# A hybrid decoder layer on one core: the softmax division of two blocks at once on GpSimd, q's square there, and the meta weights transposed in one step

## The chip, the cores and the metric

The kernel runs on one core of one Trainium2 chip. The metric is the device time of one execution in microseconds (us). A core has five engines that run side by side, each through its own instructions in order: TensorE (PE; PEld is its weight load), VectorE (DVE), ScalarE (ACT), GpSimd (POOL) and SyncE (SP), which here only starts transfers. They wait for each other through semaphores.

## The reference, cut to what matters here

A layer of 1024 tokens with 16 meta tokens ahead of them: attention and a state-space scan side by side, merged by gates, then a feed-forward part. The change is in the attention, which works on blocks of 128 tokens. Each block looks at the 16 meta tokens, the block before it and itself.

```python
q = rmsnorm(q.reshape(b, L, N_Q_HEADS, HEAD_DIM), q_norm[i])      # 16 heads of 64, 4 for each of 4 k/v heads
k_win = jnp.concatenate([meta k, k_prev, kb], axis=2)             # 16 + 128 + 128 columns
s = jnp.einsum('bnqkrd,bnskd->bnkrqs', qb, k_win) * scale         # masked by the window
m = jnp.maximum(jnp.max(s, axis=-1, keepdims=True), sink)
e = jnp.exp(s - m)
p = e / (jnp.sum(e, axis=-1, keepdims=True) + jnp.exp(sink - m))
o_r = jnp.einsum('bnkrqs,bnskd->bnqkrd', p, v_win)
```

## The kernel before

The program is written in the order of the algorithm. A scheduler puts the instructions of each engine in an order of its own, by their priorities (an instruction written later has less) and by when its own model of times thinks that operands and buffers are there. After that the order on an engine is fixed.

The attention loop (L734 to L740) runs over 32 steps i = kv * 8 + b: for each of the 4 k/v heads the 8 blocks of 128 tokens, each with 4 query heads. Five stages are called in each turn, with a lead in steps: `q_proj` 10, `values` 0, `p_turn` 1, `scores` 4, `q_turn` 6.

- `q_proj` (L609): 24 matmuls of 256 columns into `q`. ScalarE squares them into `qsq` (L619) and copies them into `qp` (L620), VectorE sums the squares by head into `qss` (L621). Every fourth block `rsqrt` (L146) makes 13 small VectorE instructions on 16 numbers (L151 to L159).
- `q_turn` (L628): GpSimd scales q into `qn` (L633), TensorE transposes it, ScalarE and VectorE split it into `qs`, the rounded part and the rest (L645, L648). At a new k/v head `k_prep` (L583) does the same for the keys (`kh`, `kl`).
- `scores` (L652): two matmuls for each head into `s`, then one VectorE instruction (L663) that adds the mask, writes `pr` and leaves the smallest negated value in `mn`. ScalarE takes the exponentials and their sums `den` (L669). VectorE makes `es`, adds it to `den` and takes the reciprocal, four numbers each (L667, L672, L673). Then the weights are divided: heads 0 and 1 on VectorE (L675), heads 2 and 3 on GpSimd in one instruction (L677). `pr` has three buffers.
- `p_turn` (L681): eight transposes of `pr` (`ptp` for the block before, `ptc` for the own one), split by ScalarE and VectorE into `ph` and `pl` (L199, L200). The 16 meta columns are split on GpSimd into `pm` (L701, L702), 48 columns a head with a gap of zeros, transposed head by head (`ptm`, four matmuls), and copied to `pmt` (L707).
- `values` (L710): products with v into `o`, five matmuls of 512 columns, the last with the meta weights, 48 rows high (L720). ScalarE and VectorE join the halves in `av` (L725, L726), and SyncE stores it to `at_d` (L728).

Between the blocks the gate units `g` (24 matmuls of 512 columns, L540) run: four ahead of the loop and one after each of the steps 22, 27 and 31. Weights are split in halves by `w_cols` (L107), the lower half (`wl_q`, `wl_g`, L104) on GpSimd. Behind the loop the memory of attention is given back, SyncE loads `W` (L765), the scan runs on VectorE (L784 to L794), and TensorE runs the other gate units (L767, L798).

Of the kernel before, what the change touches and what calls it, by code (L numbers as in the profile page):

```python
# [46 lines left out]
def hybrid_layer_kernel(ctx: ExitStack, tc: tile.TileContext, x, meta_tokens, norm_mix, w_in, q_norm, k_norm,  # L47
# [174 lines left out]
    vm = kvp.tile([48, NKV, 2, HD], F32R, name="vm")  # L222
# [6 lines left out]
    with sbuf("p1", 2) as p1:  # L229
# [73 lines left out]

        nc.vector.memset(vm.bitcast(F32), 0.0)
        split(vm[0:16, :, 0], vm[0:16, :, 1], o[:NMETA, 256:512].rearrange("p (h d) -> p h d", d=HD))
        nc.vector.tensor_copy(vm[32:48], vm[0:16])
# [252 lines left out]
    with sbuf("ag", 1, "right") as ag, sbuf("at", 2) as at:  # L559
# [12 lines left out]
        pms = []  # L572

# [6 lines left out]

        kt = {}

        def k_prep(kv):  # L583
# [3 lines left out]
            c0 = kv * HD  # L587

# [20 lines left out]
        def q_proj(i):  # L609
# [16 lines left out]
        qst, probs, pts = {}, {}, {}  # L626
# [25 lines left out]
        def scores(i):  # L652
# [4 lines left out]
            mn = at.tile([P, 4], F32, tag="mn", name=f"mn{i}")  # L657
            for h in range(4):
                o = bank(f"s{i}_{h}", "s")
                for j in range(2):  # L660
# [3 lines left out]
                                               scalar=nsink[:, kv * 4 + h:kv * 4 + h + 1], op0=ALU.add, op1=ALU.min, accum_out=mn[:, h:h + 1])  # L664
            es = at.tile([P, 4], F32, tag="es", name=f"es{i}")
            den = at.tile([P, 4], F32, tag="den", name=f"den{i}")
            nc.vector.tensor_tensor(out=es, in0=mn, in1=nsink[:, kv * 4:kv * 4 + 4], op=ALU.subtract)  # L667
            for h in range(4):
                nc.scalar.activation(out=pr[:, h, :n], in_=pr[:, h, :n], func=AF.Exp, scale=-1.0,  # L669
                                     bias=mn[:, h:h + 1], accum_out=den[:, h:h + 1])  # L670
# [3 lines left out]
            for h in range(2):  # L674
                nc.vector.tensor_scalar(out=pr[:, h, :n], in0=pr[:, h, :n], scalar1=den[:, h:h + 1], scalar2=None,  # L675
                                        op0=ALU.mult)
            nc.gpsimd.tensor_tensor(out=pr[:, 2:4, :n], in0=pr[:, 2:4, :n],  # L677
                                    in1=den[:, 2:4].unsqueeze(2).to_broadcast([P, 2, n]), op=ALU.mult)
            probs[i] = pr

        def p_turn(i):  # L681
# [15 lines left out]
            if i < 2:  # L697
                pms.append(one([P, 4, 48], F32R, f"pm{i}"))
                nc.gpsimd.memset(pms[i].bitcast(F32), 0.0)
            pm, src = pms[i % 2], pr[:, :, cm:cm + 16]  # L700
            nc.gpsimd.tensor_copy(pm[:, :, 0:16], src)  # L701
            nc.gpsimd.tensor_tensor(out=pm[:, :, 32:48], in0=src, in1=pm[:, :, 0:16].bitcast(F32), op=ALU.subtract)  # L702
            pt = bank(f"ptm{i}", "x")
            for h in range(4):
                nc.tensor.transpose(pt[:48, h * P:h * P + P], pm[:, h, :].bitcast(F32), ident)
            pmt = at.tile([48, 512], F32R, tag="pmt", name=f"pmt{i}")
            nc.scalar.copy(pmt, pt[:48])  # L707
            pts[i] = parts, pmt

        def values(i):  # L710
            kv, b = divmod(i, 8)
            c0 = kv * HD
# [3 lines left out]
            for k, (kb, ph, pl) in enumerate(parts):  # L716
                nc.tensor.matmul(o, v2[:, kb, kv].rearrange("p a d -> p (a d)"), ph, start=(k == 0), stop=False)
            for kb, ph, pl in parts:
                nc.tensor.matmul(o[:64, :], v2[:, kb, kv, 0, :], pl, start=False, stop=False)
            nc.tensor.matmul(o, vm[:, kv].rearrange("p a d -> p (a d)"), pm, start=False, stop=True)  # L720
# [575 lines left out]
```

## Time and profile before

| | |
|---|---|
| Time, median of 3 runs | 1693.79 us (1693.68 to 1696.36) |
| The profiled execution | 1697.95 us |
| Its span, first to last instruction | 1696.2 us, granted TensorE clock 0.975 |
| TensorE busy | 1586.7 us, 94% of the span |
| VectorE busy | 1181.0 us, 70% |
| ScalarE busy | 695.7 us, 41% |
| GpSimd busy | 372.4 us, 22% |
| Chain that ended last | TensorE 59%, VectorE 14% of the span |

The shares are averages over stages that have different limits. Matmuls are pipelined, so that the busy time of TensorE includes their overlap; how fast it runs is read from how many it issues in a stretch. Times in the rows count from the span's start. A wait is put down to what released it.

### The profile page before, as it was taken

The numbers are of one execution on the slowest core, as the hardware profiler recorded it, in microseconds if no ns is written. First come the engines' busy times: TensorE is split into PE (matmuls) and PEld (weight loads), VectorE is DVE, ScalarE is ACT, GpSimd is POOL, SyncE is SP. The second block draws the span as 40 slices with busy tenths as digits, with TensorE's granted clock in tenths as the row PEclk, the third lists the DMA queues.
The fourth block names the chain that finished last, engine by engine and source line by source line (L and its number), as shares of the span: only waits on it lengthen the run. The fifth ranks groups of instructions, "written<-read, shape, count | busy, mean of one in ns | idle before, by whom it ended". The sixth has DMA issues, their size and how long they took to land.

```text
span 1696.2 us, 22168 instructions
## 1 busy us (share of the span) xinstructions
PE 1586.7 (94%) x8002; PEld 1318.3 (78%) x8002; DVE 1181.0 (70%) x2280; ACT 695.7 (41%) x1363; POOL 372.4 (22%) x277
## 2 busy tenths in 40 slices
PE   7999888989989999799998897999999999799999
PEld 5788768778867888788887785788888888678787
DVE  7779885999995798732217688865656665399763
ACT  4433425878885421442212333533333333243230
POOL 0000112243321001113323200111111121265441
PEclk9999989999999999999999997999999999999999
DMA  5254442011012874742213341423223331584431
GB/s 190 61 130 133 134 143 74 24 38 45 20 51 60 311 218 131 212 130 75 74 51 104 111 163 57 143 87 106 94 94 116 107 106 56 199 305 159 147 109 75
DMA packets 175359, 196.93 MB, mean 116 GB/s; under 512 B 12769, under 2 KB 125409, under 8 KB 175121
## 3 DMA queue, kind: packets, MB, share of 16 engines
q1 hardware_dynamic: 166736, 183.94, 33.6%
q10 hardware_dynamic: 8288, 11.01, 2.1%
q8 instruction: 63, 1.03, 0.3%
q0 software_dynamic: 224, 0.56, 0.1%
q14 instruction: 48, 0.39, 0.1%
HBM read 140.62 MB, written 54.85 MB: 115 GB/s over the span
## 4 chain that ended last, share of the span: by engine, by line
PE 59%; DVE 14%; DMA 4%; ACT 3%; issue 3%; SPq 0%; POOL 0%; ACTq 0%; DVEq 0%
PE ch_fg L907 6%; PE ch_fu L907 6%; PE ch L907 6%; PE za L122 5%; PE wo L122 5%; PE zb L122 5%; PE si L907 4%; PE g L122 3%; PE th_fg L907 3%; PE th_fu L907 3%; PE q L122 2%; PE si_fg L907 2%; PE si_fu L907 2%; DVE pr L663 1%; DVE cm L207 1%
## 5 line engine op out<-in xcount | busy, mean ns | idle before, releaser
L122 PE MATMUL g<-xn,wh_g 128*128 128x512 f32 x512 | 165.4, 403 | 0.1
L907 PE MATMUL ch<-B,A 128*128 128x512 f32 x528 | 127.2, 398 | 13.8 <-ACT B L1228 7.4
L907 PEld LDWEIGHTS ch<-B,A 128*128 128x128 f32 x528 | 100.7, 192 | 37.7 <-ACT B L1228 7.8
L122 PEld LDWEIGHTS g<-xn,wh_g 128*128 128x128 f32 x512 | 97.2, 192 | 22.7 <-PE s L661 0.3
L122 PE MATMUL q<-wh_q,xn 128*128 128x256 f32 x512 | 105.3, 293 | 5.4 <-ACT qp L620 5.4
L122 PE MATMUL g<-xn,wl_g 128*128 128x512 f32 x256 | 102.2, 399 | 0.0
L907 PE MATMUL si<-B,A 128*128 128x512 f32 x396 | 92.6, 389 | 0.5 <-DVE h2o L911 0.5
L122 PE MATMUL wo<-wh_o,mt 128*128 128x512 f32 x256 | 83.9, 406 | 9.3 <-DVE h L984 4.9
L122 PE MATMUL u<-xn,wh_u 128*128 128x272 f32 (+2 forms) x384 | 92.4, 334 | 0.0
L122 PEld LDWEIGHTS q<-wh_q,xn 128*128 128x128 f32 x512 | 85.1, 196 | 7.0 <-ACT qp L620 5.8
L907 PEld LDWEIGHTS si<-B,A 128*128 128x128 f32 x396 | 74.3, 188 | 16.3 <-issue 0.9
L911 POOL TENSOR_TENSOR a<-c,c_fg 128x512 f32<-128x512 f32 x10 | 15.9, 1586 | 315.0 <-DVE c L911 211.1
L858 DVE TENSOR_TENSOR ssm<-za,zs 128x512 f32<-128x512 f32 x16 | 11.0, 690 | 105.3 <-ACT zs L857 105.3
L1228 ACT CAST A<-rawa 128x1536 fp32r<-128x1536 f32 (+1 forms) x28 | 38.5, 1374 | 99.7 <-issue 49.4
L122 PE MATMUL zb<-zt,wh_zb 128*128 128x512 f32 x256 | 79.3, 390 | 0.0
L122 PE MATMUL za<-zt,wh_za 128*128 128x512 f32 x256 | 79.2, 390 | 0.0
L122 PE MATMUL q<-wl_q,xn 128*128 128x256 f32 x256 | 74.5, 291 | 0.0
L911 DVE TENSOR_TENSOR A<-rawa,A 128x1536 fp32r<-128x1536 f32 (+1 forms) x28 | 65.4, 2334 | 12.5 <-ACT A L1228 12.5
L911 POOL TENSOR_TENSOR B<-t,B 128x1536 fp32r<-128x1536 f32 (+1 forms) x16 | 60.2, 3774 | 54.5 <-ACT B L1228 54.5
L669 ACT ACTIVATE pr<-pr,mn 128x272 f32<-128x272 f32 (+1 forms) x128 | 64.8, 507 | 16.5 <-DVE mn L663 14.0
L122 PEld LDWEIGHTS u<-xn,wh_u 128*128 128x128 f32 x384 | 66.7, 198 | 5.5
L122 PEld LDWEIGHTS wo<-wh_o,mt 128*128 128x128 f32 x256 | 50.0, 196 | 20.5 <-DVE h L984 5.3
(426 smaller groups left out, 4211.6 us busy)
## 6 DMA issues: line engine op xcount, KB each, us to landing
rawa<-act_d SPq DMA_DIRECT2D x21, 768.0 KB
raw_fg<-in_w_ffn_in_dram SPq DMA_DIRECT2D x20, 512.0 KB
raw_fu<-in_w_ffn_in_dram SPq DMA_DIRECT2D x20, 512.0 KB
rawb<-in_w_ffn_out_dram SPq DMA_DIRECT2D x6, 1536.0 KB
act_d<-a SPq DMA_DIRECT2D x33, 256.0 KB
raw_g<-in_w_in_dram SPq DMA_DIRECT2D x16, 512.0 KB
act_d<-c_fg SPq DMA_DIRECT2D x30, 256.0 KB
u_d<-uf SPq DMA_DIRECT2D x64, 65.0 KB
```

The source lines that it names most:

```text
L122: nc.tensor.matmul(o, lhs(kb, a), rhs(kb, b), start=(kb == 0 and i == 0), stop=(kb == n - 1 and i == 2))
L207: nc.vector.tensor_tensor(out=m, in0=v, in1=a[:, 2 * k:2 * k + 2, g0:g0 + 4].unsqueeze(3) .to_broadcast([P, 2, 4, n]), op=ALU.mult)
L663: nc.vector.tensor_tensor_reduce(out=pr[:, h, :n], in0=o[:, :n], in1=mask, scale=1.0, scalar=nsink[:, kv * 4 + h:kv * 4 + h + 1], op0=ALU. ...
L669: nc.scalar.activation(out=pr[:, h, :n], in_=pr[:, h, :n], func=AF.Exp, scale=-1.0, bias=mn[:, h:h + 1], accum_out=den[:, h:h + 1])
L858: nc.vector.tensor_tensor(out=dst, in0=oa, in1=sg, op=ALU.mult)
L907: nc.tensor.matmul(o, lhs(kb, a), rhs(kb, b), start=(first and kb == 0 and i == 0), stop=(kb == n - 1 and i == 2), skip_group_check=not first)
L911: eng.tensor_tensor(out=out, in0=in0, in1=in1, op=op)
L1228: nc.scalar.copy(hi, src)
```

## The change

- The division by `den` waits for two blocks (an even one and the odd one after it). `mn`, `es` and `den` are tiles of 2 x 4 numbers, `es`, the addition and the reciprocal run once for the pair, and GpSimd then divides all four heads of the first and of the second block, one instruction each. VectorE divides nothing.
- q's square is taken on GpSimd from `qp`, and VectorE scales its sums by 1/64 once for four blocks.
- The meta weights of the four heads lie side by side in `pm` (4 x 2 x 16 columns, the rounded part and the rest), and one transpose turns them. In `values` each head then multiplies them with a tile `vms` of v's meta rows that is zero outside the rows of this head: four matmuls of 128 columns. GpSimd fills `vms` at each new k/v head from `v1`, whose second half a DMA on GpSimd's queue copies.
- The lower part of the weights, `pl`, is multiplied with both halves of v (128 columns instead of 64).
- All stages but `q_proj` get a priority 1000 higher.

```diff
+        vms = [one([P, 4, 2, HD], F32R, f"vm{i}") for i in range(2)]
+        for vm in vms:
+            nc.gpsimd.memset(vm.bitcast(F32), 0.0)
...
+            for h in range(4):
+                nc.gpsimd.tensor_copy(vms[kv % 2][32 * h:32 * h + 32, h], v1[:, kv])
...
-            nc.scalar.activation(out=sq, in_=o[:, 0:256], func=AF.Square, scale=0.125)
-            nc.scalar.copy(qp[i // 4][:, b % 4, :], o[:, 0:256])
+            q_ = qp[i // 4][:, b % 4, :]
+            nc.scalar.copy(q_, o[:, 0:256])
+            nc.gpsimd.tensor_tensor(out=sq, in0=q_, in1=q_, op=ALU.mult)
...
-                qr[i // 4] = rsqrt(qss.pop(i // 4), P, 16, at, f"q{i}")
+                ms = qss.pop(i // 4)
+                nc.vector.tensor_scalar(out=ms, in0=ms, scalar1=1.0 / HD, scalar2=None, op0=ALU.mult)
+                qr[i // 4] = rsqrt(ms, P, 16, at, f"q{i}")
...
+            if b % 2 == 0:
+                sums[i // 2] = [at.tile([P, 2, 4], F32, tag=t, name=f"{t}{i}") for t in ("mn", "es", "den")]
+            mn, es, den = sums[i // 2]
...
+            probs[i] = pr
+            if b % 2 == 0:
+                return
...
-            for h in range(2):
-                nc.vector.tensor_scalar(out=pr[:, h, :n], in0=pr[:, h, :n], scalar1=den[:, h:h + 1], scalar2=None,
-                                        op0=ALU.mult)
-            nc.gpsimd.tensor_tensor(out=pr[:, 2:4, :n], in0=pr[:, 2:4, :n],
-                                    in1=den[:, 2:4].unsqueeze(2).to_broadcast([P, 2, n]), op=ALU.mult)
-            probs[i] = pr
+            for k in range(2):
+                pr, n = probs[i - 1 + k], window(b - 1 + k)[1]
+                nc.gpsimd.tensor_tensor(out=pr[:, :, :n], in0=pr[:, :, :n],
+                                        in1=den[:, k].unsqueeze(2).to_broadcast([P, 4, n]), op=ALU.mult)
...
-            for h in range(4):
-                nc.tensor.transpose(pt[:48, h * P:h * P + P], pm[:, h, :].bitcast(F32), ident)
-            pmt = at.tile([48, 512], F32R, tag="pmt", name=f"pmt{i}")
-            nc.scalar.copy(pmt, pt[:48])
+            nc.tensor.transpose(pt[:, 0:P], pm.bitcast(F32).rearrange("p h a k -> p (h a k)"), ident)
+            pmt = at.tile([P, P], F32R, tag="pmt", name=f"pmt{i}")
+            nc.scalar.copy(pmt, pt[:, 0:P])
...
-            nc.tensor.matmul(o, vm[:, kv].rearrange("p a d -> p (a d)"), pm, start=False, stop=True)
+            for h in range(4):
+                nc.tensor.matmul(o[:, h * P:h * P + P], vms[kv % 2][:, h].rearrange("p a d -> p (a d)"), pm, start=False,
+                                 stop=True, skip_group_check=True)
...
-                    f(i + ahead)
+
+                    with ExitStack() as first:
+                        if f is not q_proj:
+                            first.enter_context(tc.high_priority(1000))
+                        f(i + ahead)
```

How the scheduler lays this out is seen at two places in the middle of attention. A name's number is its step, so `pr10` is the weights of step 10. GpSimd before, at the division of steps 10 and 11 (`pm0` and `pm1` were two tiles used in turn):

```order
L677 TENSOR_TENSOR pr10_3809<-pr10_3809,den10_3828 128x544
L701 CAST pm0_2959<-pr10_3809 128x4x16
L702 TENSOR_TENSOR pm0_2959<-pr10_3809,pm0_2959 128x4x16
L633 TENSOR_TENSOR qn15_4173<-qp12_3246,rs_i_q15_3633 128x256
L677 TENSOR_TENSOR pr11_3909<-pr11_3909,den11_3928 128x544
L701 CAST pm1_3068<-pr11_3909 128x4x16
L702 TENSOR_TENSOR pm1_3068<-pr11_3909,pm1_3068 128x4x16
```

GpSimd with the change, at the same two steps (here and below its lines are those of the changed program; L688 is the division, L708 and L709 make `pm`, L623 is q's square, L638 makes `qn`):

```order
L688 TENSOR_TENSOR pr10_3770<-pr10_3770,den10_3773 128x1088
L688 TENSOR_TENSOR pr11_3864<-pr11_3864,den10_3773 128x1088
L708 CAST pm10_4082<-pr10_3770 128x4x16
L638 TENSOR_TENSOR qn16_4251<-qp16_3699,rs_i_q19_4035 128x256
L638 TENSOR_TENSOR qn17_4357<-qp16_3699,rs_i_q19_4035 128x256
L623 TENSOR_TENSOR qsq20_4153<-qp20_4126 128x256
L709 TENSOR_TENSOR pm10_4082<-pr10_3770,pm10_4082 128x4x16
L708 CAST pm11_4190<-pr11_3864 128x4x16
L623 TENSOR_TENSOR qsq21_4286<-qp20_4126 128x256
L709 TENSOR_TENSOR pm11_4190<-pr11_3864,pm11_4190 128x4x16
```

The division of a step was followed at once by its `pm`. Now both divisions of a pair come first, and two `qn` and a square lie between the first and the second half of `pm10`.

TensorE before, at the scores of step 13 (L661), which take over the `pr` buffer of step 10:

```order
L661 MATMUL s13_1_4148<-kh1_3347,qs13_3945 128x272
L661 MATMUL s13_1_4148<-kl1_3348,qs13_3945 128x272
L717 MATMUL o9_4103<-php9_3994,v2_112 128x512
L717 MATMUL o9_4103<-phc9_4003,v2_112 128x512
L719 MATMUL o9_4103<-plp9_3995,v2_112 64x512
L719 MATMUL o9_4103<-plc9_4004,v2_112 64x512
L720 MATMUL o9_4103<-pmt9_4014,vm_114 128x512
L639 MATMUL qT15_4175<-ident_87,qn15_4173 128x128 x2
L661 MATMUL s13_2_4152<-kh1_3347,qs13_3945 128x272
L661 MATMUL s13_2_4152<-kl1_3348,qs13_3945 128x272
L122 MATMUL q20_4185<-wh_q2_0_3729,xn10_0_104 128x256
```

TensorE with the change, at the first scores of the same step, and then from `ptm10` on (`ptm`: the meta transpose, L711; L726: the meta product):

```order
L668 MATMUL s13_0_4090<-kh1_3314,qs13_3896 128x272
L668 MATMUL s13_0_4090<-kl1_3315,qs13_3896 128x272
L668 MATMUL s13_1_4094<-kh1_3314,qs13_3896 128x272
L668 MATMUL s13_1_4094<-kl1_3315,qs13_3896 128x272
L122 MATMUL q20_4128<-wh_q2_0_3689,xn10_0_104 128x256
L122 MATMUL q20_4128<-wl_q2_0_3690,xn10_0_104 128x256
```

```order
L723 MATMUL o10_4157<-plc10_4079,v2_112 128x512
L711 MATMUL ptm10_4085<-ident_87,pm10_4082 128x128
L701 MATMUL ptp11_4172<-ident_87,pr11_3864 128x128 x4
L701 MATMUL ptc11_4181<-ident_87,pr11_3864 128x128 x4
L668 MATMUL s13_2_4098<-kh1_3314,qs13_3896 128x272
L668 MATMUL s13_2_4098<-kl1_3315,qs13_3896 128x272
L668 MATMUL s13_3_4102<-kh1_3314,qs13_3896 128x272
L668 MATMUL s13_3_4102<-kl1_3315,qs13_3896 128x272
L726 MATMUL o10_4157<-pmt10_4087,vm1_2305 128x128 x4
L723 MATMUL o11_4290<-php11_4177,v2_112 128x512
```

The last two heads of step 13 have moved behind the transposes of step 11, while q's projection 20 starts beside the scores of step 13 in both. `ptm10` is now one matmul.

## Rows read from the trace of the kernel before

**Rows 1.** Instructions of one tile, `q`: count, ns min/median/max, first and last start.

```profile
L122 PE MATMUL q<-wh_q,xn x512: 274/281/580, 258.9 to 474.0; 128*128 128x256 f32 x171
```

**Rows 2.** Timeline of SyncE, 300 to 560 us: start, length of the merged run.

```profile
311.20 46.44 SPq L728 DMA_DIRECT2D at_d<-av  x5
...
537.19 11.50 SPq L728 DMA_DIRECT2D at_d<-av  x3
548.85 0.34 SPq L765 DMA_DIRECT2D W<-v_d  x1
```

**Rows 3.** Windows: busy us of each engine in a stretch (instructions), granted clock.

```profile
core 0: us, PE busy (x) PEld busy (x) DVE busy (x) ACT busy (x) POOL busy (x), PEclk, DMA share, GB/s
355.00:535.00 180.00, 166.41 (x1079) 135.62 (x1079) 166.64 (x544) 150.76 (x423) 58.55 (x97) 0.98 0.15 43
...
546.00:683.00 137.00, 137.00 (x607) 111.38 (x607) 111.16 (x260) 36.29 (x49) 6.05 (x3) 1.00 0.64 213
```

**Rows 4.** Chain that ended last: start, us, what; TensorE's runs in attention and after.

```profile
324.44 0.44 PE ptc L691 x4
...
369.42 2.85 PE q L122 x24
...
535.15 0.55 PE ptm L705 x4
...
546.60 33.41 PE g L122 x143
```

**Rows 5.** Waits, 255 to 550 us: who for whom, total us, times, longest.

```profile
POOL pr L677 <- DVE den L673: 54.5, 16, 8.7
...
PEld o L720 <- issue: 11.3, 30, 0.4
```

**Rows 6.** Groups by shape, 290 to 545 us: count | busy us, mean ns | idle before.

```profile
L677 POOL TENSOR_TENSOR pr<-pr,den 128x544 f32<-128x544 f32 x28 | 32.1, 1147 | 68.6 <-DVE den L673 37.8 <-DVE rs_q_q L157 8.1 <-DVE pr L675 6.0
...
L675 DVE TENSOR_SCALAR pr<-pr,den 128x272 f32<-128x272 f32 x56 | 30.4, 583 | 0.4
...
L707 ACT CAST pmt<-ptm 48x512 fp32r<-48x512 f32 x32 | 18.5, 578 | 0.8 <-PE ptm L705 0.5
L633 POOL TENSOR_TENSOR qn<-qp,rs_i_q 128x256 f32<-128x256 f32 x29 | 17.7, 618 | 40.1 <-PE qT L639 21.6 <-DVE rs_i_q L159 8.4 <-DVE den L672 4.8
...
L702 POOL TENSOR_TENSOR pm<-pr,pm 128x64 fp32r<-128x64 f32 x32 | 10.3, 321 | 2.3
...
L619 ACT ACTIVATE qsq<-q 128x256 f32<-128x256 f32 x25 | 9.6, 383 | 2.8 <-PE q L122 2.3
...
L701 POOL CAST pm<-pr 128x64 fp32r<-128x64 f32 x32 | 8.5, 264 | 17.1 <-DVE pr L675 13.1 <-DVE rs_q_q L158 1.2 <-PE ptm L705 0.7
...
L667 DVE TENSOR_TENSOR es<-mn,nsink 128x4 f32<-128x4 f32 x32 | 7.9, 248 | 0.4
L672 DVE TENSOR_TENSOR den<-den,es 128x4 f32<-128x4 f32 x32 | 7.4, 232 | 0.2
...
L673 DVE RECIPROCAL den<-den 128x4 f32<-128x4 f32 x32 | 5.4, 168 | 0.2
```

**Rows 7.** Timeline of GpSimd and VectorE, 345 to 360 us: start, us.

```profile
349.75 2.35 POOL L104 TENSOR_TENSOR wl_q<-raw_q,wh_q 128x1024 fp32r<-128x1024 f32 x1 [1.85 <-ACT wh_q L103]
352.58 1.09 POOL L677 TENSOR_TENSOR pr<-pr,den 128x544 f32<-128x544 f32 x1 [0.47 <-DVE den L673]
353.63 2.41 POOL L104 TENSOR_TENSOR wl_q<-raw_q,wh_q 128x1024 fp32r<-128x1024 f32 x1
...
349.79 2.33 DVE L672 TENSOR_TENSOR den<-den,es 128x4 f32<-128x4 f32 x1
...
352.53 3.66 DVE L675 TENSOR_SCALAR pr<-pr,den 128x272 f32<-128x272 f32 x2
```

**Rows 8.** Small VectorE instructions in attention: count, ns min/median/max, first and last start.

```profile
L672 DVE TENSOR_TENSOR den<-den,es x32: 144/154/2327, 299.9 to 526.4; 128x4 f32<-128x4 f32 x32
...
L154 DVE TENSOR_SCALAR rs_i_q<-rs_i_q x8: 136/170/2316, 279.2 to 485.7; 128x16 int32<-128x16 int32 x8
```

More of the change, by code (lines that the diff above doesn't have):

```diff
@@ L302, in hybrid_layer_kernel @@
             nc.vector.tensor_tensor(out=k, in0=k, in1=kr[:n, b].unsqueeze(2).to_broadcast([n, NKV, HD]), op=ALU.mult)
-        nc.vector.memset(vm.bitcast(F32), 0.0)
-        split(vm[0:16, :, 0], vm[0:16, :, 1], o[:NMETA, 256:512].rearrange("p (h d) -> p h d", d=HD))
-        nc.vector.tensor_copy(vm[32:48], vm[0:16])
+        split(v1[0:16, :, 0], v1[0:16, :, 1], o[:NMETA, 256:512].rearrange("p (h d) -> p h d", d=HD))
+        nc.gpsimd.dma_start(out=v1[16:32], in_=v1[0:16])
         def tt(o, a, b, op=ALU.mult, eng=None):
@@ L663, in scores @@
                 nc.vector.tensor_tensor_reduce(out=pr[:, h, :n], in0=o[:, :n], in1=mask, scale=1.0,
[L664 to L667, printed above, removed]
+                                               scalar=nsink[:, kv * 4 + h:kv * 4 + h + 1], op0=ALU.add, op1=ALU.min,
+                                               accum_out=mn[:, b % 2, h:h + 1])
             for h in range(4):
                 nc.scalar.activation(out=pr[:, h, :n], in_=pr[:, h, :n], func=AF.Exp, scale=-1.0,
-                                     bias=mn[:, h:h + 1], accum_out=den[:, h:h + 1])
+                                     bias=mn[:, b % 2, h:h + 1], accum_out=den[:, b % 2, h:h + 1])
+            probs[i] = pr
+            if b % 2 == 0:
+                return
+            del sums[i // 2]
+            nc.vector.tensor_tensor(out=es, in0=mn, in1=nsink[:, kv * 4:kv * 4 + 4].unsqueeze(1).to_broadcast([P, 2, 4]),
+                                    op=ALU.subtract)
             nc.scalar.activation(out=es, in_=es, func=AF.Exp)
@@ L695, in p_turn @@
                 parts.append((kb, ph, pl))
[L697 to L702, printed above, removed]
+            pm, src = at.tile([P, 4, 2, 16], F32R, tag="pm", bufs=1, name=f"pm{i}"), pr[:, :, cm:cm + 16]
+            nc.gpsimd.tensor_copy(pm[:, :, 0], src)
+            nc.gpsimd.tensor_tensor(out=pm[:, :, 1], in0=src, in1=pm[:, :, 0].bitcast(F32), op=ALU.subtract)
             pt = bank(f"ptm{i}", "x")
[L704 to L707 removed]
+            nc.tensor.transpose(pt[:, 0:P], pm.bitcast(F32).rearrange("p h a k -> p (h a k)"), ident)
+            pmt = at.tile([P, P], F32R, tag="pmt", name=f"pmt{i}")
+            nc.scalar.copy(pmt, pt[:, 0:P])
             pts[i] = parts, pmt
@@ L716, in values @@
             for k, (kb, ph, pl) in enumerate(parts):
-                nc.tensor.matmul(o, v2[:, kb, kv].rearrange("p a d -> p (a d)"), ph, start=(k == 0), stop=False)
-            for kb, ph, pl in parts:
-                nc.tensor.matmul(o[:64, :], v2[:, kb, kv, 0, :], pl, start=False, stop=False)
-            nc.tensor.matmul(o, vm[:, kv].rearrange("p a d -> p (a d)"), pm, start=False, stop=True)
+                for j, p_ in enumerate((ph, pl)):
+                    nc.tensor.matmul(o, v2[:, kb, kv].rearrange("p a d -> p (a d)"), p_, start=(k + j == 0),
+                                     stop=(k == len(parts) - 1 and j == 1))
+            for h in range(4):
+                nc.tensor.matmul(o[:, h * P:h * P + P], vms[kv % 2][:, h].rearrange("p a d -> p (a d)"), pm, start=False,
+                                 stop=True, skip_group_check=True)
             av = at.tile([P, 2, P], F32, tag="av", name=f"av{i}")
```

7 lines of the change are left out of this document (2 added, 5 removed).

## The prediction, made before the changed kernel had run

> **What bounds the kernel now.** I read the windows first, to find the stage that the change touches, then the stores and waits inside it, then the groups of instructions, and the timeline for the odd long ones.
>
> The stage is attention, from q's first matmul at 258.9 us [rows 1] to the last store of `av`, issued by 548.7 us, after which SyncE at once issues the load of `W` for the scan [rows 2]. From 546 to 683 us TensorE has no gap at all (137.00 of 137) [rows 3]: it runs gate units, 143 matmuls in 33.41 us to begin with [rows 4]. The scan on VectorE hangs on the load of `W`. So both things that follow begin where attention ends, and I take every microsecond saved there one to one off the end.
>
> Inside attention, between the fifth store (issued by 357.64) and the last (548.69), 27 blocks take 191 us: **7.08 us a block, 14.2 a pair** [rows 2]. From 355 to 535 us VectorE is busy 166.64 of 180 us, ScalarE 150.76, GpSimd 58.55 [rows 3]. Per block that is 6.55, 5.93 and 2.30 us. TensorE's busy time is no measure, since matmuls overlap, so I add what a block issues: q's projection 24 matmuls in 2.85 us, transposes 0.44 for four, the meta transposes 0.55 for four [rows 4]; 8 score matmuls of about 0.12 (as one of q's, 2.85/24), two transposes of `qn` at 0.11, five value matmuls of 512 columns at 0.234 (33.41/143), and before the meta one a gap of 11.3/30 = 0.38 that only the issue explains [rows 5]. Sum 2.85 + 0.96 + 0.22 + 0.88 + 1.17 + 0.38 + 0.55 = 7.0 us for a block that has its projection beside it. So VectorE is the bound, and TensorE stands right behind it. That caps what relief of VectorE can bring.
>
> **The change, part by part.**
>
> *Division of the first two heads leaves VectorE.* 56 instructions, busy 30.4 us together [rows 6]. Neighbours on VectorE overlap by some 0.07 us each, so about 27 us of its time goes (the 8 of the first blocks are half as wide and left out). Much of this was waiting: at 352.53 two of them last 3.66 us while GpSimd runs its own division (1.09) and a weight split (2.41) [rows 7].
>
> *`es`, `den` and reciprocal once for two blocks.* 7.9 + 7.4 + 5.4 = 20.7 us [rows 6]; the instructions handle 8 numbers instead of 4, so half goes: 10, less overlap 9. The scaling of q's sums adds 8 small ones of 0.17, 1.4 us [rows 8]. VectorE: 27 + 9 - 1.4 = **35 us less, 1.1 a block: 6.55 to 5.45**.
>
> *ScalarE* loses 32 squares at 383 ns (12.3 us) and half of `es`; the copy of the meta weights shrinks from 48x512 (578 ns) to 128x128. With the 128x256 square as the nearest row, (578 - 383)/256 gives 0.76 ns a column and so 0.29 us, 9 us in all [rows 6]. 5.93 falls to about 5.2 a block.
>
> *TensorE.* One meta transpose instead of four: 0.55 to 0.14. The meta product becomes four matmuls of 128 columns; the nearest rows are the transposes, 0.11 each, 0.44 against 0.234 + 0.38 if the gap goes with the 48-row shape that it stands before. So 0.58 less, 7.0 to **6.4 a block**. If the gap stays, 6.8.
>
> *GpSimd.* Its division goes from 544 to 1088 elements a partition. 256 cost 618 ns and 544 cost 1147: 1.84 ns an element, so **2.15 us** each. q's square is as large as `qn`: 0.62 [rows 6]. 2.30 + 1.0 + 0.62 + 0.1 (the copies of v's meta rows) = 4.0 us a block; it is not the bound. No row shows one of 1088 elements; the bounds are 2.0 (the slope alone) and 2.56 (a weight split takes 2.41 us for 1024 elements [rows 7]), and I take 2.15, since the rows it comes from are of the same instruction and type.
>
> *What takes the place of the wait.* GpSimd waited 54.5 us for `den` [rows 5]; now others wait for GpSimd. `pr` has three buffers, and a pair holds two until its division. So the scores of block 13 need the buffer of block 10, which is free only when GpSimd has divided 10 **and** 11 and made `pm10`; the order puts two `qn` and a square between the halves of `pm10`. In time: 2 x 2.15 + 0.26 + 0.62 x 3 + 0.32 = 6.7 us [rows 6]. Pairs with nothing between take 4.9, the pair 14/15, with two weight splits between, 10.2; over the pairs the mean is 5.9. From there to the next reciprocal VectorE has in a row four score rows of about 0.42, two `pl` of 0.6, four more score rows, `es`, two `qs` of 0.48, one `av`, `den`: 6.3 us (estimate from their spacing on the timeline). The loop is 5.9 + 6.3 = **12.2 us a pair**, under 14.2 and above VectorE's 10.9.
>
> *Priority.* It does little: in the order q's projection 20 stands beside the scores of block 13 both before and after. I give it nothing.
>
> *The sum.* TensorE needs 12.8 a pair while projections run and less after; the loop 12.2. Neither is met exactly by queues that are served in order, so I take 13.0 a pair: 1.2 x 13.5 pairs = 16 us less from the fifth block on. The start gets its first division only after the second block's scores (+4) and loses the locked divisions (3.66 - 0.6, and others like it: -4); the end gains 2 us of latency, under gate matmuls for TensorE but not for the load of `W`, and the last blocks pay back as much by the smaller meta work. Sum **-16 us**. Against the profiled execution, 1697.95 becomes 1682; it lies 4 us above the median of the runs, so the median 1693.8 becomes **1678**.
>
> **A rule that speaks against it.** At 349.79 a `den` of four numbers takes 2.33 us instead of the usual 0.15, over by the time that GpSimd's split of 349.75 ends [rows 7, 8]. The Trainium skill (SBUF — State Buffer, "Who interferes with whom") says that a VectorE instruction with two SBUF inputs and a GpSimd instruction that reads SBUF exclude each other for the whole instruction; the trace agrees. By that rule the third rival below is what the change does; without it the sum above stands.
>
> **The rivals.**
> 1. *Full relief.* Queues fill well, the gap goes, and the last blocks follow VectorE's 10.9: 2.2 to 2.8 less a pair, 30 to 38 us: 1656 to 1664. For it: ScalarE and GpSimd are far from full. Against: TensorE's 6.4 a block.
> 2. *The buffer loop becomes the bound, slower than before.* Place: the scores of block 13, which wait for `pm10`, while `ptp10` and the last scores of the block before stand in TensorE's queue behind a projection of 24 matmuls. It breaks even where the loop grows by 2.0 us to 14.2. A whole projection ahead of it makes 12.2 + 2.85 = 15.05: 0.85 x 13.5 = +11, 1705. A division at its upper bound adds only 0.8 and does not do it alone. For it: every stage is served in order, and a pair now waits for its later block. Against: the projections stand mostly where TensorE has nothing else to do.
> 3. *The lock.* Of `es` and `den` 32 remain, and 8 x 14 of the rsqrt, that read SBUF alone; before, one of 8 at line 154 took 2316 ns instead of 170, and `den` averages 232 instead of 154 [rows 6, 8]. GpSimd's share of the stage goes from 32% (2.30 of 7.08) to 60% (4.0 of 6.5) and its pieces double. If each rsqrt chain is stopped twice for 1.1 us or more, 8 x 2.2 = 18 us, the gain is gone: 1690 to 1696. Against: `es` and `den` come when GpSimd is waiting for them.
> 4. *It does not do what it says* is settled for the priority alone, above.
>
> **How the numbers follow.** Forecast (1667 to 1688) 52%, full relief 18%, lock 14%, buffer loop 16%. The time is the forecast's, 1678. The range reaches from full relief's end, 1656, to just beyond the lock's, 1698: left out are most of the buffer loop and a little below. A measurement of this kernel tells 0.2%, 3.4 us, from no change. Faster: 52 + 18 + 5 of the lock = 75%. Same: 9% of the lock. Slower: 16%.
>
> **What would show it.** Right: line 675's work gone from VectorE, its busy share in the stage under 90%, GpSimd's division near 2.15 us, stores of `av` about 6.5 us apart, the last before 535 us, and the same 137 us of gapless TensorE behind it. Buffer loop: VectorE idle before score rows with `pm` as releaser. Lock: `den` or rsqrt instructions of 1 us and more. The forecast is wrong if the stage after does not move with the last store, or if TensorE's clock falls in new gaps.

## The result, and the profile after

The change made the kernel **slower**: 1732.19 us (median, 1729.48 to 1736.2) against 1693.74 of the kernel before (1690.38 to 1696.36), a ratio of 1.0234, 95% interval 1.0218 to 1.0251. That is 38 us more where 16 us less had been forecast, and outside the range. The profiled execution took 1733.34 us, its span is 1731.6 us at a granted TensorE clock of 0.958 (before 1696.2 and 0.975).

SyncE's timeline of the changed kernel, 300 to 600 us (start, length of the merged run), answers to [rows 2]:

```profile
325.95 24.22 SPq L735 DMA_DIRECT2D at_d<-av  x4
365.01 67.04 SPq L735 DMA_DIRECT2D at_d<-av  x9
...
499.77 57.45 SPq L735 DMA_DIRECT2D at_d<-av  x8
564.81 16.10 SPq L735 DMA_DIRECT2D at_d<-av  x3
581.07 0.34 SPq L776 DMA_DIRECT2D W<-v_d  x1
```

The first store is issued 15 us later than before (325.95 against 311.20), the load of `W` 32 us later (581.07 against 548.85). What follows `W` takes 1150.5 us, before 1147.4. So attention holds 32 of the 35 us by which the span grew. The first 21 blocks take as long as before (499.77 - 325.95 = 174 us, before 486.81 - 311.20 = 176, both over 8 us a block). But the last eleven stores still come 8.1 us apart, from 499.77 to 580.91, where the same eleven had come 6.2 us apart before, from 486.81 to 548.69:

```profile
486.81 39.97 SPq L728 DMA_DIRECT2D at_d<-av  x8
```

Windows of the changed kernel (busy us of PE, PEld, DVE, ACT, POOL, then the granted clock), against [rows 3]:

```profile
core 0: us, PE busy (x) PEld busy (x) DVE busy (x) ACT busy (x) POOL busy (x), PEclk, DMA share, GB/s
...
355.00:535.00 180.00, 155.46 (x1022) 136.75 (x1020) 141.35 (x440) 130.07 (x375) 86.25 (x114) 0.93 0.12 36
...
515.00:535.00 20.00, 14.11 (x63) 10.99 (x62) 11.81 (x36) 14.49 (x45) 7.82 (x10) 0.77 0.09 27
535.00:555.00 20.00, 16.31 (x77) 12.55 (x77) 12.68 (x41) 13.19 (x40) 6.09 (x11) 0.80 0.05 14
555.00:583.00 28.00, 28.00 (x138) 23.05 (x137) 8.04 (x19) 9.76 (x22) 5.89 (x6) 1.00 0.26 76
```

And one window of the kernel before:

```profile
515.00:535.00 20.00, 19.41 (x97) 14.44 (x95) 15.47 (x45) 14.86 (x40) 5.38 (x10) 1.00 0.21 60
```

VectorE was relieved: 141 us of 180 against 167. But no other engine took over as the bound: TensorE is at 86%, ScalarE at 72%, GpSimd at 48%. That points to a chain through several engines. The groups of the changed kernel, 290 to 577 us (busy us, mean ns | idle time before), against [rows 6], show that the division, the dearest part of the chain, had been priced about right:

```profile
L688 POOL TENSOR_TENSOR pr<-pr,den 128x1088 f32<-128x1088 f32 x28 | 55.5, 2002 | 47.8 <-DVE den L685 38.5 <-DVE rs_i_q L153 6.9 <-DVE qss L628 2.4
...
L151 DVE TENSOR_SCALAR rs_xe_q<-qss 128x16 f32<-128x16 f32 x7 | 5.0, 716 | 0.1
...
L681 DVE TENSOR_TENSOR es<-mn,nsink 128x8 f32<-128x8 f32 x16 | 3.6, 228 | 0.2
```

The division takes 2.00 us (forecast 2.15, bounds 2.0 to 2.56), and GpSimd waits 38.5 us in these groups for `den`.

**How long a pair takes.** The first and the last of GpSimd's sixteen pairs of divisions, and below them in the kernel before the first two blocks and the last one:

```profile
310.70 3.10 POOL L688 TENSOR_TENSOR pr<-pr,den 128x576 f32<-128x576 f32 x2 [0.34 <-DVE den L685]
...
557.40 3.96 POOL L688 TENSOR_TENSOR pr<-pr,den 128x1088 f32<-128x1088 f32 x2 [5.65 <-DVE den L685]
```

```profile
300.79 0.67 POOL L677 TENSOR_TENSOR pr<-pr,den 128x288 f32<-128x288 f32 x1 [3.79 <-ACT qs L645]
...
309.36 1.21 POOL L677 TENSOR_TENSOR pr<-pr,den 128x544 f32<-128x544 f32 x1 [0.59 <-ACT pr L669]
...
526.94 1.20 POOL L677 TENSOR_TENSOR pr<-pr,den 128x544 f32<-128x544 f32 x1 [0.80 <-DVE den L673]
```

That is (557.40 - 310.70)/15 = **16.45 us a pair**, where the prediction had a loop of 12.2 and a pace of 13.0. A pair starts when its second block is ready; counted from second block to second block the kernel before has (526.94 - 309.36)/15 = 14.5. One turn of the loop late in attention, on four engines. GpSimd (start, us):

```profile
514.12 3.11 POOL L688 TENSOR_TENSOR pr<-pr,den 128x576 f32<-128x576 f32 x2 [2.46 <-DVE den L685]
517.18 0.24 POOL L708 CAST pm<-pr 128x64 fp32r<-128x64 f32 x1
519.15 0.61 POOL L638 TENSOR_TENSOR qn<-qp,rs_i_q 128x256 f32<-128x256 f32 x1 [1.74 <-PE qT L644]
519.72 0.32 POOL L709 TENSOR_TENSOR pm<-pr,pm 128x64 fp32r<-128x64 f32 x1
...
531.04 3.96 POOL L688 TENSOR_TENSOR pr<-pr,den 128x1088 f32<-128x1088 f32 x2 [9.15 <-DVE den L685]
```

TensorE in the same turn:

```profile
514.14 0.40 PE L723 MATMUL o<-plc,v 128*128 128x512 f32 x1
...
514.95 0.28 PE L668 MATMUL s<-kl,qs 128*128 128x272 f32 x1
...
515.19 0.29 PE L668 MATMUL s<-kl,qs 128*128 128x272 f32 x1
...
518.66 0.41 PE L644 MATMUL qT<-ident,qn 128*128 128x128 f32 x2 [2.67 <-DVE qs L653]
519.45 0.80 PE L723 MATMUL o<-phc,v 128*128 128x512 f32 x1 [0.38 <-DVE av L733]
...
520.98 1.06 PE L701 MATMUL ptp<-ident,pr 128*128 128x128 f32 x4
521.83 1.06 PE L701 MATMUL ptc<-ident,pr 128*128 128x128 f32 x4
522.54 0.58 PE L668 MATMUL s<-kh,qs 128*128 128x272 f32 x1
...
523.89 0.54 PE L668 MATMUL s<-kh,qs 128*128 128x272 f32 x1
```

VectorE:

```profile
520.60 0.50 DVE L670 CUSTOM_DVE_ANT_0 pr<-s,m_odd,nsink 128x272 f32<-128x272 f32 x1
...
523.38 0.50 DVE L670 CUSTOM_DVE_ANT_0 pr<-s,m_odd,nsink 128x272 f32<-128x272 f32 x1 [1.85 <-PE s L668]
...
524.69 0.50 DVE L670 CUSTOM_DVE_ANT_0 pr<-s,m_odd,nsink 128x272 f32<-128x272 f32 x1 [0.20 <-PE s L668]
...
527.25 0.15 DVE L681 TENSOR_TENSOR es<-mn,nsink 128x8 f32<-128x8 f32 x1
...
529.31 0.50 DVE L670 CUSTOM_DVE_ANT_0 pr<-s,m_even,nsink 128x272 f32<-128x272 f32 x1
...
530.30 0.17 DVE L684 TENSOR_TENSOR den<-den,es 128x8 f32<-128x8 f32 x1
...
530.71 0.19 DVE L685 RECIPROCAL den<-den 128x8 f32<-128x8 f32 x1
```

And ScalarE's one instruction on `es`:

```profile
527.83 0.21 ACT L683 ACTIVATE es<-es 128x8 f32<-128x8 f32 x1
```

Read from the top. The scores of the odd block's first two heads stand finished from 515.23 and 515.48. Their rows on VectorE begin only at 520.60. The buffer that `pr` needs is free at 520.04: behind both divisions, and behind the second half of `pm` at 519.72, which stood in GpSimd's order behind a `qn` that waited 1.74 us for TensorE. The last half microsecond is an `av` that VectorE has begun by then. The scores of the other two heads stand in TensorE's order behind the eight transposes `ptp` and `ptc`, of which four take 0.85 us from start to start (520.98 to 521.83; 0.44 in [rows 4]), so their rows come at 523.38 and 524.69. ScalarE has `es` ready at 528.04, but `den` stands in VectorE's order behind three score rows of the *next* block, two `qs` and an `av`, and comes at 530.30. Only then can GpSimd divide again. From division to first score row 6.5 us (estimated 5.9), from there to the end of the reciprocal at 530.90 10.3 us (estimated 6.3).

The groups of waits, 255 to 585 us (who for whom, total us, times, longest), show these pauses all along attention (GpSimd's wait for `den` alone would prove nothing, [rows 5] had 54.5 us of it; VectorE's for the scores was 2.4 us before):

```profile
POOL pr L688 <- DVE den L685: 42.0, 11, 9.2
...
POOL pm L708 <- PE ptm L711: 26.4, 14, 4.4
...
DVE pr L670 <- PE s L668: 18.9, 16, 2.8
...
DVE pr L670 <- POOL pm L709: 0.5, 1, 0.5
```

The sign that the prediction named for the buffer loop, VectorE idle before score rows with `pm` as the releaser, stands there only once, with 0.5 us. VectorE has other work in its order until the buffer is free, or waits for scores that stand late on TensorE. So the rows alone don't show that the buffers hold the pace; that takes the runs below.

### The profile page after: what moved, and what is told of

Read it like the earlier page. It is cut to its first block, busy times and chain, and to the rows that moved or that the text cites. A ratio compares the mean times of both kernels' runs of the same rounds, so it can differ in the third digit from the quotient of the medians.

```text
span 1731.6 us, 22018 instructions
## 1 busy us (share of the span) xinstructions
PE 1599.6 (92%) x8002; PEld 1341.4 (77%) x8002; DVE 1153.4 (67%) x2174; ACT 676.1 (39%) x1315; POOL 419.5 (24%) x326
## 4 chain that ended last, share of the span: by engine, by line
PE 69%; DVE 17%; DMA 5%; ACT 4%; issue 3%; SPq 1%; POOL 0%; DVEq 0%; ACTq 0%; POOLq 0%
PE ch_fg L918 6%; PE ch_fu L918 6%; PE ch L918 6%; PE g L122 6%; PE wo L122 5%; PE za L122 5%; PE si L918 5%; PE zb L122 5%; DVE ops L307 4%; PE th_fg L918 3%; PE th_fu L918 3%; PE q L122 3%; PE kv L122 2%; DVE cm L207 2%; PE u L122 2%
## 5 line engine op out<-in xcount | busy, mean ns | idle before, releaser
L1239 ACT CAST A<-rawa 128x1536 fp32r<-128x1536 f32 (+1 forms) x28 | 38.5, 1374 | 100.3 <-issue 49.1
L688 POOL TENSOR_TENSOR pr<-pr,den 128x1088 f32<-128x1088 f32 (+1 forms) x32 | 60.0, 1895 | 51.3 <-DVE den L685 42.0
```

The lines of the kernel that those rows point to most:

```text
L688: nc.gpsimd.tensor_tensor(out=pr[:, :, :n], in0=pr[:, :, :n], in1=den[:, k].unsqueeze(2).to_broadcast([P, 4, n]), op=ALU.mult)
L1239: nc.scalar.copy(hi, src)
```

## The experiments

Theory A: the pair holds two of three `pr` buffers until its later block, and the loop through GpSimd, TensorE, ScalarE and VectorE sets the pace. Rivals: the priority or the start; the single `pm` buffer, for which GpSimd now waits 26.4 us; the lock between VectorE and GpSimd. Ratios are to the kernel before, run on the same chip, with 95% intervals.

**The priority.** One run takes it out of the changed kernel, one puts it alone into the kernel before, and one takes it from the first `q_turn` only.

```diff
-                    with ExitStack() as first:
-                        if f is not q_proj:
-                            first.enter_context(tc.high_priority(1000))
-                        f(i + ahead)
+                    f(i + ahead)
```

> The changed kernel with all stages at one priority, nothing else different. Start theory (the priority puts the first k_prep ahead of q's copies on ScalarE, where it waits for the store of vs): the first copy of q starts near 263 us instead of 274.8, attention ends 8 to 12 us earlier, 1720 to 1724 us in all, and the last eleven blocks stay as slow as with the change (about 8 us apart). Rival (the priority spoils the order of the whole stage, the tail too): 1690 to 1700 us, with the last blocks back at 6 us.

Measured 1733.53, ratio 1.023 (1.0205 to 1.0255): nothing comes back, though the first copy of q starts at 263.99 again. Both expectations missed.

> The kernel before, with the priority added and nothing else. Start theory: ScalarE waits 9 us for the store of vs with q's copies behind it, 1700 to 1706 us. Rival (the priority is harmless by itself and only hurts with the pairs): 1690 to 1697.

Measured 1694.91, ratio 1.0011 (0.9996 to 1.0025): harmless by itself.

```diff
-                        if f is not q_proj:
+                        if f is not q_proj and (f is not q_turn or i + ahead):
```

> The changed kernel, only the very first q_turn (with the first k_prep) at normal priority. Start theory: the same 8 to 12 us as without any priority, 1720 to 1724. Rival (the later stages' priority is what costs): no change, 1730 to 1734.

Measured 1726.53, ratio 1.0189 (1.0163 to 1.0214), some 6 to 8 us better than the changed kernel. In the changed kernel ScalarE waits 9.5 us for a transfer of `v_d`, with the first copies of `qp` behind it at 274.83; here it waits 5.5 us, and the copies start at 262.34. The run without any priority had that too and gained nothing, so the 6 to 8 us are not explained by it. The first store still comes at 324.25, so the late start of the stores is mostly not this wait.

**Pair or single block.** The changed kernel with `es`, `den` and division block by block, all four heads on GpSimd:

```diff
-            if b % 2 == 0:
-                sums[i // 2] = [at.tile([P, 2, 4], F32, tag=t, name=f"{t}{i}") for t in ("mn", "es", "den")]
-            mn, es, den = sums[i // 2]
+            mn, es, den = (at.tile([P, 4], F32, tag=t, name=f"{t}{i}") for t in ("mn", "es", "den"))
...
-            for k in range(2):
-                pr, n = probs[i - 1 + k], window(b - 1 + k)[1]
-                nc.gpsimd.tensor_tensor(out=pr[:, :, :n], in0=pr[:, :, :n],
-                                        in1=den[:, k].unsqueeze(2).to_broadcast([P, 4, n]), op=ALU.mult)
+            nc.gpsimd.tensor_tensor(out=pr[:, :, :n], in0=pr[:, :, :n],
+                                    in1=den.unsqueeze(2).to_broadcast([P, 4, n]), op=ALU.mult)
```

> The changed kernel, but es, den, reciprocal and the division run for each block by itself, all four heads on GpSimd. Buffer theory (a pair holds two of the three pr buffers until both are divided): the last eleven blocks fall from 8.2 to about 6 us each and the middle gains a little, 1700 to 1715 us. Lock theory (small VectorE instructions wait for GpSimd's divisions): twice as many of them and as much GpSimd work, so no gain or a loss, 1732 to 1745.

Measured 1694.02, ratio 1.0004 (0.9988 to 1.0021): the loss of 38 us is gone with the pairing. The reverse, the kernel before with the pairing alone (division split between VectorE and GpSimd as before, but held for two blocks):

> The kernel before, with es, den and reciprocal for two blocks and the division held back until then, divided as before (two heads on VectorE, two on GpSimd); nothing else of the change. pr theory (a pair holds two of three buffers): slower although 9 us of small VectorE work is gone, 1710 to 1740 us, VectorE's busy share of the stage down. Rival (pairs are only bad with the long GpSimd divisions): 1680 to 1692.

Measured 1723.55, ratio 1.0171 (1.0135 to 1.0207). Pairing costs 29 us without any other part of the change; its divisions start at 308.79 and 554.39, 16.4 us a pair.

**The buffers.** A fourth `pr`, for which `kl` gives up its second buffer:

```diff
-            kl = at.tile([P, 4, 272], F32R, tag="kl", name=f"kl{kv}")
+            kl = at.tile([P, 4, 272], F32R, tag="kl", bufs=1, name=f"kl{kv}")
...
-            pr = at.tile([P, 4, 272], F32, tag="pr", bufs=3, name=f"pr{i}")
+            pr = at.tile([P, 4, 272], F32, tag="pr", bufs=4, name=f"pr{i}")
```

> The changed kernel with four buffers for pr instead of three (to make room, one kl instead of two, which can only cost, at three changes of the k/v head). pr theory: the scores no longer wait for the division of a whole pair, 1700 to 1715 us, the last eleven blocks about 6.5 us apart. pm theory: no gain, 1730 to 1740.

Measured 1696.86, ratio 1.0028 (1.001 to 1.0047): 35 us come back with the pairs still in place. Its first and last pair of divisions on GpSimd:

```profile
310.40 3.10 POOL L688 TENSOR_TENSOR pr<-pr,den 128x576 f32<-128x576 f32 x2 [0.34 <-DVE den L685]
...
524.11 3.96 POOL L688 TENSOR_TENSOR pr<-pr,den 128x1088 f32<-128x1088 f32 x2 [2.23 <-DVE den L685]
```

The first is where it was (310.70), the last 33 us earlier: 14.25 us a pair, and the last pair waits 2.23 us for `den`, not 5.65 as in the changed kernel. With the two runs before it this shows the cause: a pair in three buffers. Whether the buffers act as waits or through the order that the scheduler lays for three or four of them, the runs don't separate.

The rival that GpSimd's wait of 26.4 us for the one `pm` buffer matters: `pm` gets two. To make room the next runs have one tile `vms`, which changes the output (the last blocks of a k/v head are multiplied with the meta rows of v of the next head; the work is the same).

```diff
-        vms = [one([P, 4, 2, HD], F32R, f"vm{i}") for i in range(2)]
+        vms = [one([P, 4, 2, HD], F32R, f"vm{i}") for i in range(1)]
...
-            pm, src = at.tile([P, 4, 2, 16], F32R, tag="pm", bufs=1, name=f"pm{i}"), pr[:, :, cm:cm + 16]
+            pm, src = at.tile([P, 4, 2, 16], F32R, tag="pm", bufs=2, name=f"pm{i}"), pr[:, :, cm:cm + 16]
```

> The changed kernel with two buffers for pm instead of one (to make room, one vms tile instead of two, which the next k/v head has to wait for). pm theory (GpSimd stands at pm until the transpose of the pm before is through, with qn, squares and divisions behind it, 26 us of waits): 1712 to 1720 us. pr theory (the pair holds pr): under 5 us gained, 1727 to 1734.

Measured 1731.86, ratio 1.0229 (1.0176 to 1.0282): the 12 to 20 us expected of `pm` are not there. A long wait in the table was not on the chain. With four `pr` as well, and with single blocks:

> The changed kernel with both, four pr and two pm (one kl, one vms). If both hold it up: 1690 to 1705 us, below either alone. If pairs cost by something else than buffers: above 1720.

> The one-block division (e4) with two buffers for pm and one vms. pm theory: 5 to 12 us below e4's 1694, 1682 to 1689. If the one buffer of pm only hurts pairs: the same as e4, 1691 to 1697.

Measured 1704.2, ratio 1.0064 (1.0044 to 1.0085), and 1689.91, ratio 0.9995 (0.9978 to 1.0012). Neither is a gain: the first is 7 us slower than four `pr` with one `pm`, the second stands to its kernel before about as the single block with one `pm` did (1.0004).

**Does the division's length count in the loop?** The changed kernel, with heads 0 and 1 left undivided, so that GpSimd's instruction is half as long:

```diff
-                nc.gpsimd.tensor_tensor(out=pr[:, :, :n], in0=pr[:, :, :n],
-                                        in1=den[:, k].unsqueeze(2).to_broadcast([P, 4, n]), op=ALU.mult)
+                nc.gpsimd.tensor_tensor(out=pr[:, 2:4, :n], in0=pr[:, 2:4, :n],
+                                        in1=den[:, k, 2:4].unsqueeze(2).to_broadcast([P, 2, n]), op=ALU.mult)
```

> The changed kernel, but GpSimd divides only heads 2 and 3 of the two blocks (heads 0 and 1 are left undivided): the two divisions take 2.3 us a pair instead of 4.0, nothing else changes. Theory A (a chain through the three pr buffers sets the pace in attention): the chain is 1.7 us shorter over some 14 pairs, about 20 us less than the changed kernel, 1710 to 1716, and the stores in the tail 7.3 us a block instead of 8.2. Theory B (order on TensorE or its lower granted clock sets the pace, and the division lies beside it): within 5 us of the changed kernel, 1728 to 1735.

Measured 1695.97, ratio 1.0025 (1.0008 to 1.0042): 36 us less than the changed kernel, more than the 20 expected. Its divisions start at 311.92 and 530.00, 14.5 us a pair: 1.9 less, where the two instructions are 1.8 shorter (3.96 to 2.14). That is what a chain through the division would give, nearly one to one, and 15 x 1.9 = 29 us. The rest stays open; the scheduler, which plans with its own times, also laid the orders on the engines anew, so that this run is not the halved division alone.

**Where is the gain that VectorE's relief should bring?** Without the loop the changed kernel only equals the one before. Two runs on the kernel before: heads 0 and 1 left undivided (the relief, and nothing for GpSimd), and all heads divided on GpSimd block by block (the relief and its price).

```diff
             for h in range(2):
                 nc.vector.tensor_scalar(out=pr[:, h, :n], in0=pr[:, h, :n], scalar1=den[:, h:h + 1], scalar2=None,
                                         op0=ALU.mult)
```

> The kernel before without VectorE's division: heads 0 and 1 are left undivided, GpSimd divides heads 2 and 3 as before. It shows what the relief of VectorE is worth where GpSimd gets nothing more to do. Theory A (VectorE bounds attention, TensorE stands close behind): 14 to 20 us less, 1674 to 1680. Theory B (orders in the queues and TensorE set the pace, VectorE's busy time does not): within 5 us of before, 1689 to 1694. If this one gains and the division on GpSimd alone does not, GpSimd's added work is what ate the relief.

Measured with these three lines left out: 1680.49, ratio 0.9922 (0.9897 to 0.9946), 12 to 13 us less. VectorE's groups there, 258 to 552 us:

```profile
L667 DVE TENSOR_TENSOR es<-mn,nsink 128x4 f32<-128x4 f32 x32 | 9.0, 282 | 0.6
...
L159 DVE SCALAR_TENSOR_TENSOR rs_i_q<-rs_q_q,rs_i_q 128x16 f32<-128x16 f32 x24 | 5.9, 244 | 0.3
...
L157 DVE TENSOR_TENSOR rs_q_q<-rs_i_q 128x16 f32<-128x16 f32 x24 | 4.4, 185 | 0.2
```

> The kernel before, and of the change only this: GpSimd divides all four heads of each block in one instruction of 1088 elements, block by block; VectorE divides nothing. Theory A (the relief of VectorE is worth its 27 us only as far as VectorE sets the pace, and GpSimd's longer use of SBUF gives part back by stretching small VectorE instructions): 1685 to 1694, with es and the instructions at lines 157 to 159 at 300 to 400 ns instead of 165 to 248. Theory B (relief counts in full, and e4 lost it again to the start, q's square or the priority): 1665 to 1675. Theory C (GpSimd's latency ahead of the transposes becomes the wait): over 1700.

Measured with the division of all four heads as one GpSimd instruction: 1694.81, ratio 1.0 (0.9983 to 1.0017). The gain is all gone. The same groups:

```profile
L667 DVE TENSOR_TENSOR es<-mn,nsink 128x4 f32<-128x4 f32 x32 | 13.6, 424 | 0.3
...
L159 DVE SCALAR_TENSOR_TENSOR rs_i_q<-rs_q_q,rs_i_q 128x16 f32<-128x16 f32 x24 | 9.6, 398 | 0.3
L157 DVE TENSOR_TENSOR rs_q_q<-rs_i_q 128x16 f32<-128x16 f32 x24 | 8.0, 332 | 0.4
```

One of them on its timeline, VectorE and then GpSimd:

```profile
489.44 1.85 DVE L667 TENSOR_TENSOR es<-mn,nsink 128x4 f32<-128x4 f32 x1
```

```profile
489.27 2.00 POOL L674 TENSOR_TENSOR pr<-pr,den 128x1088 f32<-128x1088 f32 x1 [3.22 <-DVE den L673]
```

An `es` of four numbers, usually 0.16 us, ends as the division of 489.27 ends. All small VectorE groups together (`es`, `den`, the reciprocal and L151 to L159) are busy 61.8 us here and 48.0 without GpSimd's added part. So stretched instructions are there. Whether they are what ate the gain is another question, since each division also holds the transposes 0.9 us longer; this pair of runs doesn't separate the two.

The third engine that could divide is ScalarE. Head 0 moved there in the kernel before, nothing else:

```diff
-            for h in range(2):
-                nc.vector.tensor_scalar(out=pr[:, h, :n], in0=pr[:, h, :n], scalar1=den[:, h:h + 1], scalar2=None,
-                                        op0=ALU.mult)
+            nc.scalar.activation(out=pr[:, 0, :n], in_=pr[:, 0, :n], func=AF.Copy, scale=den[:, 0:1])
+            nc.vector.tensor_scalar(out=pr[:, 1, :n], in0=pr[:, 1, :n], scalar1=den[:, 1:2], scalar2=None, op0=ALU.mult)
```

> The kernel before, and of the division head 0 goes from VectorE to ScalarE (a copy with den as its factor), head 1 stays on VectorE, heads 2 and 3 on GpSimd. VectorE loses 28 x 0.58 = 16 us, ScalarE gains about as much (0.52 a block, 5.9 to 6.4), GpSimd nothing. Theory A (relief of VectorE counts where GpSimd gets nothing for it): about half of the 13 us that leaving both heads undivided gave, 1684 to 1689. Theory B (ScalarE, which has the exponentials and the splits in the same chain, passes its added work on): 1691 to 1700.

Measured **1684.38**, ratio 0.994 (0.9916 to 0.9964): the one version with the whole output that beats both kernels. Its groups, 258 to 552 us:

```profile
L675 DVE TENSOR_SCALAR pr<-pr,den 128x272 f32<-128x272 f32 x28 | 16.0, 571 | 0.3
L674 ACT ACTIVATE pr<-pr,den 128x272 f32<-128x272 f32 x28 | 14.5, 517 | 0.7 <-DVE den L673 0.5
L667 DVE TENSOR_TENSOR es<-mn,nsink 128x4 f32<-128x4 f32 x32 | 8.1, 254 | 0.3
```

ScalarE pays 0.52 us a block and small VectorE instructions keep their length (the same groups come to 43.8 us). So the longer division on GpSimd gave the relief back, not the mere move to another engine, though this run moves one head and not two. It also shows that VectorE's busy time alone does not set the pace. From 258 to 552 us it is 236.93 us here and 237.15 with all four heads on GpSimd, against 249.94 in the kernel before: the relief is the same, and only this run is faster.

**The meta part,** alone on the kernel before (one transpose, small products, `pl` with both halves of v), and on top of the head on ScalarE:

```diff
-            for h in range(4):
-                nc.tensor.transpose(pt[:48, h * P:h * P + P], pm[:, h, :].bitcast(F32), ident)
+            nc.tensor.transpose(pt[:, 0:P], pm.bitcast(F32).rearrange("p h a k -> p (h a k)"), ident)
```

> The kernel before, with the meta weights turned at once, the four small meta products and pl against both halves of v; nothing else of the change. If VectorE alone sets the pace there, as the prediction said: 0 to 4 us faster, 1687 to 1692. If TensorE and ScalarE set it as much: 8 to 16 us faster, 1675 to 1683.

Measured 1695.29, ratio 1.0015 (0.9991 to 1.0039): no gain.

> As the one with head 0 divided on ScalarE, and with the meta weights turned at once as in the change (one meta transpose, a copy of 128x128, four small meta products), which takes 0.3 us a block from ScalarE and some 0.6 from TensorE. Theory A: 1682 to 1688, a little below the one without it. Theory B (meta part alone gave nothing, ScalarE's added work decides): 1691 to 1700.

Measured 1696.67, ratio 1.0012 (0.9995 to 1.0029). The meta part gains nothing alone, and with it the gain of the ScalarE version is lost. Why is open: its load of `W` comes at 552.29, without the meta part at 546.92, and ScalarE waits 8.6 us for the transfer of `v_d` at the start, as it does with the meta part alone. Both runs also have one `pm` buffer where the kernel before has two tiles; no run tells these apart.

**Combinations.** The first `q_turn` without priority, with four `pr` and with single blocks:

> The changed kernel with four buffers for pr (one kl, as in e6) and the first q_turn at normal priority (as in e2). If both losses are independent: 5 to 7 us below e6's 1697, 1689 to 1692 us. If the start is hidden once the pairs flow: the same as e6, 1695 to 1698.

> The changed kernel with the division for each block by itself (as in e4) and the first q_turn at normal priority (as in e2). If both losses are independent: 5 to 7 us below e4's 1694, 1687 to 1689 us, a little below the kernel before. If not: 1692 to 1696.

Measured 1694.9, ratio 0.9999 (0.9981 to 1.0017), and 1699.99, ratio 1.0033 (1.0015 to 1.0052). The two sets of runs were on different chips, so the ratios are compared. With four `pr` the ratio goes from 1.0028 to 0.9999, some 5 us, about what the same edit gave in the changed kernel, though the two intervals just touch. With single blocks it goes from 1.0004 to 1.0033, 5 us the other way; why is open.

## Why the prediction was wrong, by its own steps

- **What bounds the kernel: right in part.** VectorE's divisions are on the path of the kernel before: with them simply left out the time falls by 12 to 13 us. But its 6.55 us a block are not the pace by themselves, since two runs with the same 237 us of VectorE work differ by 10 us. That the time after attention shifts one to one also held (1150.5 against 1147.4 us).
- **VectorE's 35 us: about right as work, not as time.** In attention its busy time fell from 249.94 (258 to 552 us) to 222.12 (258 to 583), by 28. Part of the relief went into stretched instructions (L151 716 ns, before about 214).
- **GpSimd's division: right.** 2.00 us for 2.15. Its busy time in attention grows from 92.28 us (258 to 552) to 141.80 (258 to 583), 1.55 us a block; 1.72 was forecast.
- **"What takes the place of the wait": the step that failed.** The chain was the right one, and the place too: the scores wait for a `pr` that both divisions and `pm` hold. Its size was wrong: 12.2 us a pair, measured 16.45. The half up to the first score row was 5.9 by estimate and 6.5 in the turn shown. The other half was 6.3 and came to 10.3, because it was added up as if VectorE had its instructions in a row. In fact two heads' scores stand behind the transposes of the pair's second block, a place that the order quoted ahead of the prediction already showed, and `den` stands behind three score rows, two `qs` and an `av`. Each crossing to another engine costs its place in that engine's order. With 12.2, the loop lay under the pace of before and seemed free; at 16.45 it lies above. With four buffers a pair takes 14.25 us, and the loss is gone.
- **The second rival is what happened,** a loop through the buffers that becomes the bound, with 16% as its chance. Its price of 1705 took one projection of 2.85 us as the only growth, to 15.05 a pair. But the loss is largest where the projections are over (the last one starts at 491.9): the last five pairs take 15.9 us each, before 13.1. There the loop also opens the gaps in which TensorE's granted clock falls (0.77 and 0.80 where it was 1.00), which lengthens the transposes inside it; how much of the loop this makes, no run shows. That the forecast would be wrong "if TensorE's clock falls in new gaps" was said; it had no price.
- **The start: +4 - 4, too low for the first block, but not the loss.** The first division starts at 310.70 instead of 300.79, and the first store is 15 us late. In part that is the wait for two blocks: with the division block by block and the rest of the change it starts at 304.86. But the second block of the kernel before was divided at 309.36. Of the 30 us by which the last pair is late (557.40 against 526.94), only 1.3 are there at the first pair; the other 29 are pace. The stores split the loss in another way, since the first store waits for a whole pair. With four `pr` the first store is as late (324.97), and the time is back.
- **The third rival, the lock, is there; that it is the second loss is not shown.** Its sign stands in the changed kernel (an instruction of L151, usually 0.21 us, takes up to 1.93). The runs on the kernel before show that GpSimd's division takes back what VectorE gains. But with equal VectorE busy time one of them gained and the other did not, so the longer division itself, or the place of the stretched instructions in the chain, may be the cause as well. "`es` and `den` come when GpSimd is waiting for them", the argument against it, is wrong: with several steps in flight, the `es` of one block meets the division of another.
- **Priority: right** (nothing, by the two runs that add it or take it out whole; with the first `q_turn` alone at normal priority the changed kernel was 6 to 8 us faster, for a reason that is open). **Meta products and transposes: right in size** (the copy 266 ns, estimated 290), **worth nothing in time** in the run that has them alone. That TensorE was not the bound would explain it; that run had other differences, so it is not shown.

## What to carry to other kernels

Before two items are batched, count the buffers that the pair holds until its later half, and go round the loop with each engine's order of instructions in hand: every instruction waits for what stands ahead of it, not only for its operands. An extra buffer tells in one run whether that loop is the cause. And work moved off the busiest engine gains only if the engine that takes it does not hold it up elsewhere: the same division was worth 12 to 13 us when left out, 9 to 10 when half of VectorE's share went to ScalarE, and nothing on GpSimd.

## What the runs showed of the hardware

- A GpSimd instruction of 1088 elements with two operands can hold a VectorE instruction of four numbers nearly for its whole length: `es` 1.85 us beside a division of 2.00. On average `es` went from 282 to 424 ns when GpSimd's division doubled, and stayed at 254 when the work went to ScalarE. The Trainium skill (SBUF — State Buffer, "Who interferes with whom") names a port pair that these two engines share under an exclusive lock and gives ScalarE ports of its own; the traces agree on both (on ScalarE the division kept 517 ns on average).
- TensorE's granted clock, 1.00 at 515 to 535 us before, was 0.77 there in the changed kernel, with TensorE busy 14.11 of 20 us; 0.77 is the mean of stretches at 2.4 and at 1.2 GHz. A value matmul took 0.40 us at 514.14; TensorE then stood still for 2.67 us ahead of 518.66, and the value matmul at 519.45 took 0.80. Four transposes behind it took 0.85 us instead of 0.44. From 555 us on, with gate matmuls and no gap, the clock was 1.00 again. Gaps that a chain leaves on TensorE can so lengthen the chain a second time.
